# A decoder trunk on one core: address phases of the matmul operands in SBUF

## The chip, the core and the metric

The kernel runs on one core of one Trainium2 chip. The metric is the device time of one execution in microseconds (us), from which the host is left out; the profile is one such execution, taken by the hardware profiler. A smaller number is better.

## The reference

Two decoder layers over 256 tokens of width 2048, in float32: layer 0 mixes tokens with retention (8 heads), layer 1 with sliding-window attention (32 heads, 4 of keys and values). Each mixer is followed by a SwiGLU block and by a gated per-layer embedding; one last norm ends it.

```python
for i in range(DEPTH):                       # 2 layers, 256 tokens, d = 2048
    h = rmsnorm(x, norm_mix[i])
    if i % 2 == 0:
        x = x + retention_mixer(h, ret_w_in[j], ret_gn[j], ret_w_out[j])
    else:
        x = x + swa_mixer(h, swa_w_in[j], swa_sinks[j], swa_w_out[j])
    x = x + swiglu(rmsnorm(x, norm_ffn[i]), ffn_w_in[i], ffn_w_out[i])
    gate = jax.nn.sigmoid(rmsnorm(x, norm_ple[i]) @ ple_w_gate[i])
    x = x + gate * (p[i] @ ple_w_proj[i])
return rmsnorm(x, norm_final)
```

Nearly all of the arithmetic is the projections: an activation of 256 tokens times a weight matrix that is read from HBM once.

## The kernel before, in words

Every projection is cut into chunks of 512 output columns, and each chunk into units of 256 rows of the weight (two blocks of 128 rows, 128 x 1024 values in SBUF). 928 such units go by in one fixed order, from the first projection of layer 0 to the last of layer 1, with 12 matmuls to a unit.

For a unit, four things happen on four engines. The SyncE queue loads the weights into a `raw` buffer (five of them, `load`, L130). ScalarE rounds them to float32r into a `hi` buffer (L208). VectorE puts the remainder into a `lo` buffer (L209). TensorE then multiplies (`multiply`, L141 to L161). Loads run five units ahead, the splits three units ahead (`run`, L163), and there are four `hi` and four `lo` buffers, so that the buffer of unit i + 3 is the one that unit i - 1 has left. In between, steps of side work (transposes, norms, attention) are put into the engines' queues.

The activation is the stationary operand. It too lies in two float32r parts, each transposed to [128, blocks, 256 tokens]: `xTh` and `xTl` for the residual stream (the operand of every projection that reads a norm), `pTh` and `pTl` for the embedding, and tiles of a stage's own pool for the inputs of the output projections: `yTh`/`yTl` (retention), `oTh`/`oTl` (attention), `hTh`/`hTl` (SwiGLU). For each block and each half of the tokens there are three matmuls of 128 x 128 by 128 x 512, in this order: stationary `xTh` with moving `hi` (L159), the same `xTh` with moving `lo` (L160), `xTl` with moving `hi` (L161). Each has a weight load of its own (PEld, 128 x 128), and the load for the next matmul runs while the present one streams.

Three places need a name for what follows. A tile's *phase* is its start address in the partition modulo 128 bytes. The blocks of a stationary tile are 512 bytes wide and those of a moving tile 2048 bytes, so every operand of L159 to L161 has the phase of its tile. The built program's allocation gives for the kernel before:

| tile | start, bytes | phase |
|---|---|---|
| `xTh`, `xTl` | 33952, 50336 | 32, 32 |
| `pTh`, `pTl` | 66720, 68768 | 32, 32 |
| `raw`, five | 70816 to 87200 | 32 |
| `hi`, four | 91296 to 103584 | 32 |
| `lo`, four | 107680 to 119968 | 32 |
| `yTh`, `oTh`, `hTh` (each in its stage) | 132288 | 64 |
| `yTl`, `oTl`, `hTl` | 165056, 148672, 177344 | 64 |
| `prh`, `prl`, `vh`, `vl` (retention's inner products, L350 to L352) | 209600 to 216768 | 64 |

So a projection that reads `xT` or `pT` has stationary and moving operands of one phase, and one that reads `yT`, `oT` or `hT` has its stationary operand 32 bytes further on.

Of the kernel before, what the change touches and what calls it, by code (L numbers as in the profile page):

```python
# [2 lines left out]

# [8 lines left out]
F32 = mybir.dt.float32  # L12
# [6 lines left out]
P = 128  # L19
D = 2048  # L20
S = 256
# [22 lines left out]
class Lhs:  # L44
    """A transposed activation, split exactly into two float32r parts."""

# [8 lines left out]
class Chunk:  # L55
    """512 output columns for all tokens, accumulated over the whole contraction, in pieces of
    a token tile and some of the columns."""

# [6 lines left out]
class Unit:  # L65
    """KU blocks of 128 rows of a weight, in one chunk's columns."""

# [5 lines left out]
class Stage:  # L73
    """A part of the trunk with tiles of its own, from its first unit to its last."""

# [3 lines left out]
    def linear(self, w, block, lhs, done, units=None, chunk=None):  # L79
        """One chunk: block of 512 columns of a weight laid out by `_units`."""  # L80
        ch = chunk or Chunk(self, done)
        for u in units if units is not None else range(w.shape[1]):
            self.units.append(Unit(ch, w[block, u], range(KU * u, KU * u + KU), lhs))
            ch.left += 1
# [3 lines left out]
def tile_trunk(ctx, tc, ins, out):  # L88
    nc = tc.nc
    pool = ctx.enter_context(tc.tile_pool(name="persist", bufs=1))  # L90
    wraw = ctx.enter_context(tc.tile_pool(name="wraw", bufs=5))
    whi = ctx.enter_context(tc.tile_pool(name="whi", bufs=4))
    wlo = ctx.enter_context(tc.tile_pool(name="wlo", bufs=4))
    small = ctx.enter_context(tc.tile_pool(name="small", bufs=4))
# [9 lines left out]
    turned = ctx.enter_context(tc.tile_pool(name="turned", bufs=1))  # L104
    xT = [pool.tile([P, KD, S], F32R, name=n) for n in ("xTh", "xTl")]
    pT = [pool.tile([P, PLE_K, S], F32R, name=n) for n in ("pTh", "pTl")]

    # ---------------------------------------------------------------- streams
    side = deque()

    def step_side():
# [21 lines left out]
    def split_weights(u):  # L133
        raw = u.w
        hi = whi.tile([P, KU, NW], F32R, name="hi")
        lo = wlo.tile([P, KU, NW], F32R, name="lo")
        for part in u.parts:
            split(hi[:, part, :], lo[:, part, :], raw[:, part, :])
        u.w = (hi, lo)

    def multiply(u, which, left):  # L141
        """The unit's products for some pieces of its chunk; `left` of the chunk's units are
        still to come."""
        ch = u.chunk
        need(u.lhs, u.kts)
        if ch.acc is None:
            ch.acc = []
            for n, (_, cols) in enumerate(ch.pieces):
                bank, name = (ps_acc, "acc") if n < NT else (ps_at, "at")
                ch.acc.append(bank.tile([P, NW], F32, name=name)[:, : cols.stop - cols.start])  # L150
        hi, lo = u.w
        for j, k in enumerate(u.kts):
            first = not ch.begun and j == 0
            last = left == 0 and j == KU - 1
            for n in which:
                t, cols = ch.pieces[n]
                sl = slice(t * P, (t + 1) * P)
                xh, xl = u.lhs.hi[:, k, sl], u.lhs.lo[:, k, sl]
                nc.tensor.matmul(ch.acc[n], xh, hi[:, j, cols], start=first, stop=False)  # L159
                nc.tensor.matmul(ch.acc[n], xh, lo[:, j, cols], start=False, stop=False)  # L160
                nc.tensor.matmul(ch.acc[n], xl, hi[:, j, cols], start=False, stop=last)  # L161

    def run(stages, begin):  # L163
        """All units in order, their weights AHEAD units ahead; between them, steps of side work.
        The products of the units that end the last chunk go piece by piece of its output."""
        units = [(st, u) for st in stages for u in st.units]
# [37 lines left out]

    # ------------------------------------------------------------ small pieces
    def split(hi, lo, src, scale=None):
# [9 lines left out]
    def transpose_pair(srcs):  # L216
        """Two [128, 128] blocks of both token tiles -> a PSUM tile [128, 2, S]."""
        tr = ps_tr.tile([P, 2, S], F32, name="tr")
        for j, pair in enumerate(srcs):
            for t in range(NT):  # L220
                nc.tensor.transpose(tr[:, j, t * P : (t + 1) * P], pair[t], ident)
        return tr

    def transposes(dst, src):
        """Steps that transpose src [128, NT, 512] into dst [128, 4, S], by blocks of 32 x 32."""
        n = P // SQ
        src = src.rearrange("p t (k c f) -> p t k c f", c=n, f=SQ)
        dst = dst.rearrange("p k (t c f) -> p t k c f", c=n, f=SQ)
        for i in range(n * n):
            if i % STEP == 0:  # L230
                yield
            a, b = divmod(i, n)
            nc.vector.transpose(  # L233
                dst[b * SQ : (b + 1) * SQ, :, :, a, :], src[a * SQ : (a + 1) * SQ, :, :, b, :]
            )

    def blocks(src, i):
        """Blocks 2i and 2i + 1 of 128 columns of both token tiles."""
        return [[src(t)[:, b * P : (b + 1) * P] for t in range(NT)] for b in (2 * i, 2 * i + 1)]

    class Norm:
        """Sums of squares of the residual's chunks, and the transposed residual times the gain.
        The scale by token, inv, is applied behind the product with the weights."""

# [22 lines left out]
        def places(self, c, src):  # L267
            """Steps that put a chunk's four transposed blocks in place."""
            for j in range(4):
                if j % 2 == 0:  # L270
                    yield
                self.place(4 * c + j, src[:, j, :])
# [5 lines left out]
    def residual(stage, norm, c):  # L278
        """A chunk of an output projection onto the residual, then the next norm's part."""

# [14 lines left out]

    # --------------------------------------------------------------- retention
    def retention(norm, next_norm, w_in, w_out):
# [97 lines left out]

    # ---------------------------------------------------- sliding-window attention
    def swa(norm, next_norm, w_in, w_out):
# [36 lines left out]
        def q_done_of(j):  # L434
            def q_done(acc):
# [12 lines left out]
                def scores(i):  # L448
                    """Of heads 2i and 2i + 1: the numerators and denominators' parts."""
                    ats = [ps_at.tile([P, 3 * P], F32, name="at") for _ in range(2)]  # L450
# [97 lines left out]
        for j in range(SKV):  # L548
            stage.linear(w_in, j, norm.lhs, q_done_of(j))
        # The first chunks' last units wait for the last group of heads.  # L550
        n = KD // KU
# [7 lines left out]

    # --------------------------------------------------------------------- FFN  # L560
    def ffn(layer, norm, next_norm):
# [57 lines left out]

    # --------------------------------------------------------------------- PLE  # L620
    def ple(layer, norm, next_norm, final):
# [12 lines left out]
        def pair(c):  # L634
# [3 lines left out]
            def gate_done(acc):  # L638
# [7 lines left out]
                def later():  # L646
                    # The last reads of the old operand are queued: its place is free.
                    for b, xt in enumerate(st["xt"]):
                        yield from next_norm.places(b, xt)
# [34 lines left out]
            def gate_last(acc, t, cols):  # L684
                """A piece of the last chunk; with a token tile's last one, its rows go out."""
                fin, rest, row = st["fin"], st["rest"], xs[:, t, :]
# [37 lines left out]

    # ------------------------------------------------------------------- trunk
    norms = [Norm(w, layer) for layer in range(DEPTH) for w in range(3)] + [Norm(None, 0)]
# [14 lines left out]
    def load_x():  # L741
        """The first norm's operand comes transposed, in step with the first chunk's weights."""
        for b in range(KD // KU):
# [19 lines left out]
def _constants():  # L763
    """Tables that follow from the shapes alone."""
    h = np.arange(RH, dtype=np.float64)
# [14 lines left out]
def _units(w):  # L780
    """[K, N] -> [N / 512, K / 256, 128, 2, 512]: each unit in one piece, by partitions."""
    k, n = w.shape
    return w.reshape(k // (KU * P), KU, P, n // NW, NW).transpose(3, 0, 2, 1, 4)


def _heads(w):
    """The retention's columns by heads: q and k, v, g."""
    q, k, v, g = np.split(w, [RH * RK, 2 * RH * RK, 2 * RH * RK + RH * RV], axis=1)
    parts = [a.reshape(D, RH, -1) for a in (q, k, v, g)]
    return np.concatenate(parts, axis=2).reshape(D, -1)  # L790
# [44 lines left out]
```

## Time and profile before

| what | value |
|---|---|
| time, median of 3 runs | 2649.82 us (2649.51 to 2650.46) |
| span of the profiled execution | 2647.9 us |
| TensorE busy in it | 2629.2 us, 99% |
| VectorE, ScalarE busy | 1817.2 us, 1223.7 us |
| granted TensorE clock, mean | 0.999 |
| 128 x 512 matmuls with stationary `xT` or `pT` | 7728 + 96 = 7824 |
| with stationary `yT`, `oT` or `hT` | 768 + 384 + 2112 = 3264 |
| HBM read | 493.63 MB, 187 GB/s over the span |

The profiled execution's own time is its span and what lies around it: the median of the runs is 1.9 us over the span. In the rows of the profile, a group is given by its source line, engine, operation and tiles (out<-in, with the moving operand or the stationary one first, as the program names them), then its count, its busy time and the mean duration of one instruction in ns. A matmul's duration overlaps the next one's, since matmuls are pipelined; what a matmul costs is the distance from one start to the next, which a window's length over its count of matmuls gives.

### The profile page before, as it was taken

How to read it: one execution, taken by the hardware profiler on the slowest of the kernel's cores; microseconds unless marked ns; L12 is line 12 of the kernel's file. 1: busy time of each engine (PE TensorE's matmuls, PEld its weight loads, DVE VectorE, ACT ScalarE, POOL GpSimd, SP SyncE). 2: the span in 40 equal slices, each digit the busy share in tenths (PEclk: the TensorE clock that was granted, in tenths of full speed). 3: DMA queues.
4: the chain of work that ended last, by engine and by line, in shares of the span. 5: the costliest groups of instructions: out<-in, count | busy, mean ns of one | idle time of the engine just before them, and what ended most of it. 6: DMA issues, size and time to landing. Idle time of an engine off the chain costs nothing.

```text
span 2647.9 us, 31279 instructions
## 1 busy us (share of the span) xinstructions
PE 2629.2 (99%) x11632; PEld 2142.7 (81%) x11632; DVE 1817.2 (69%) x2567; ACT 1223.7 (46%) x1527; POOL 14.6 (1%) x30
## 2 busy tenths in 40 slices
PE   8999999999999999999999999999999999999998
PEld 6888888888888888888888887777888888888887
DVE  6777777766666667676555786888757575755565
ACT  6444444444444444444444555555444444444444
POOL 0000000000000000000000000000000000000000
PEclk9999999999999999999999999999999999999999
DMA  8555555565566565656655655346666666555564
GB/s 277 185 185 186 185 186 183 181 190 184 194 192 193 191 197 190 198 186 197 190 187 187 190 193 169 121 135 202 189 198 189 197 194 194 192 188 187 189 207 144
DMA packets 140506, 497.79 MB, mean 188 GB/s; under 512 B 15809, under 2 KB 19009, under 8 KB 140225
## 3 DMA queue, kind: packets, MB, share of 16 engines
q1 hardware_dynamic: 140064, 495.73, 58.5%
q8 instruction: 91, 1.49, 0.2%
q14 instruction: 63, 0.51, 0.1%
q10 hardware_dynamic: 288, 0.07, 0.0%
HBM read 493.63 MB, written 2.10 MB: 187 GB/s over the span
## 4 chain that ended last, share of the span: by engine, by line
PE 95%; DVE 3%; issue 1%; DMA 1%; ACT 0%; SPq 0%; ACTq 0%; POOLq 0%; POOL 0%; DVEq 0%
PE acc L159 31%; PE acc L161 31%; PE acc L160 31%; DVE lo L209 1%; DVE xt L233 1%; PE at L454 1%; PE tr L506 0%; PE at L532 0%; DMA raw<-in_ret_w_in 0%; PE at L323 0%; DVE xTl L212 0%; DVE qkT L233 0%; DMA xs<-in_x 0%; PE at L350 0%; PE at L352 0%
## 5 line engine op out<-in xcount | busy, mean ns | idle before, releaser
L209 DVE TENSOR_TENSOR lo<-raw,hi 128x1024 fp32r<-128x1024 f32 (+1 forms) x929 | 1131.8, 1221 | 720.2 <-ACT hi L208 712.8
L208 ACT ACTIVATE hi<-raw 128x1024 fp32r<-128x1024 f32 (+1 forms) x929 | 982.0, 1058 | 1210.9 <-PE acc L161 1117.4
L159 PE MATMUL acc<-hi,xTh 128*128 128x512 f32 x2592 | 1011.0, 390 | 6.6 <-ACT hi L208 5.4
L161 PE MATMUL acc<-hi,xTl 128*128 128x512 f32 x2592 | 1008.0, 389 | 0.8 <-DVE xTl L212 0.6
L160 PE MATMUL acc<-lo,xTh 128*128 128x512 f32 x2592 | 1008.7, 389 | 0.0
L159 PEld LDWEIGHTS acc<-hi,xTh 128*128 128x128 f32 x2592 | 487.3, 188 | 111.6 <-ACT hi L208 5.6
L161 PEld LDWEIGHTS acc<-hi,xTl 128*128 128x128 f32 x2592 | 487.0, 188 | 103.6 <-DVE xTl L212 2.5
L160 PEld LDWEIGHTS acc<-lo,xTh 128*128 128x128 f32 x2592 | 487.3, 188 | 100.5 <-issue 0.7
L161 PE MATMUL acc<-hi,hTl 128*128 128x512 f32 x704 | 278.4, 396 | 0.0
L160 PE MATMUL acc<-lo,hTh 128*128 128x512 f32 x704 | 278.4, 395 | 0.0
L159 PE MATMUL acc<-hi,hTh 128*128 128x512 f32 x704 | 278.4, 395 | 0.0
L233 DVE STREAM_TRANSPOSE xt<-h 32x256 f32<-32x256 f32 x352 | 153.6, 436 | 6.8
L161 PEld LDWEIGHTS acc<-hi,hTl 128*128 128x128 f32 x704 | 132.2, 188 | 32.1
L160 PEld LDWEIGHTS acc<-lo,hTh 128*128 128x128 f32 x704 | 132.2, 188 | 32.1
L159 PEld LDWEIGHTS acc<-hi,hTh 128*128 128x128 f32 x704 | 132.2, 188 | 31.9
L233 DVE STREAM_TRANSPOSE xt<-xs 32x256 f32<-32x256 f32 x320 | 139.5, 436 | 6.0
L161 PE MATMUL acc<-hi,yTl 128*128 128x512 f32 x256 | 101.2, 396 | 0.0
L160 PE MATMUL acc<-lo,yTh 128*128 128x512 f32 x256 | 101.2, 395 | 0.0
L159 PE MATMUL acc<-hi,yTh 128*128 128x512 f32 x256 | 101.2, 395 | 0.0
L233 DVE STREAM_TRANSPOSE qkT<-qk 32x256 f32<-32x256 f32 x128 | 55.8, 436 | 10.2 <-ACT qk L315 8.1
L211 ACT ACTIVATE xTh<-xt,gains 128x256 fp32r<-128x256 f32 x80 | 35.8, 499 | 56.0 <-DVE xt L233 51.6
L159 PEld LDWEIGHTS acc<-hi,yTh 128*128 128x128 f32 x256 | 48.1, 188 | 11.7
(124 smaller groups left out, 1178.2 us busy)
## 6 DMA issues: line engine op xcount, KB each, us to landing
raw<-in_ffn_w_in SPq DMA_DIRECT2D x352, 512.0 KB, 4.2
raw<-in_ret_w_in SPq DMA_DIRECT2D x191, 512.0 KB, 3.6
raw<-in_ffn_w_out SPq DMA_DIRECT2D x176, 512.0 KB, 4.0
raw<-in_ret_w_out SPq DMA_DIRECT2D x64, 512.0 KB, 4.0
raw<-in_ple_w_gate SPq DMA_DIRECT2D x64, 512.0 KB, 3.8
raw<-in_swa_w_in SPq DMA_DIRECT2D x40, 512.0 KB, 3.7
raw<-in_swa_w_out SPq DMA_DIRECT2D x32, 512.0 KB, 3.7
raw<-in_ple_w_proj SPq DMA_DIRECT2D x8, 512.0 KB, 4.0
```

The costliest lines, as they stand in the source:

```text
L159: nc.tensor.matmul(ch.acc[n], xh, hi[:, j, cols], start=first, stop=False)
L160: nc.tensor.matmul(ch.acc[n], xh, lo[:, j, cols], start=False, stop=False)
L161: nc.tensor.matmul(ch.acc[n], xl, hi[:, j, cols], start=False, stop=last)
L208: nc.scalar.activation(hi, src, AF.Copy)
L209: nc.vector.tensor_tensor(lo, src, hi.bitcast(F32), op=ALU.subtract)
L211: nc.scalar.activation(hi, src, AF.Copy, scale=scale)
L233: nc.vector.transpose(dst[b * SQ : (b + 1) * SQ, :, :, a, :], src[a * SQ : (a + 1) * SQ, :, :, b, :])
L454: nc.tensor.matmul(ats[e][:, 0:P] if b == 0 else ats[e][:, P : 3 * P], qT[sl, i, b * P : (b + 1) * P], kT[sl, j, 0 : (b + 1) * P], start=True,
```

## The change

Only addresses change. The `hi` and `lo` buffers leave their rotating pools and become eight fixed tiles, used in turn by a counter (the pools also handed out four buffers in turn). Small tiles that nothing reads are put between them as pads: 96 bytes ahead of `xTh`, 32 bytes between `xTh` and `xTl`, and 32 bytes behind each `hi` buffer. On every engine the instructions, their order and the semaphores that each waits for are those of before; docstrings and some comments go too, and L159 becomes L169, L208 becomes L218.

```diff
     pool = ctx.enter_context(tc.tile_pool(name="persist", bufs=1))
     wraw = ctx.enter_context(tc.tile_pool(name="wraw", bufs=5))
-    whi = ctx.enter_context(tc.tile_pool(name="whi", bufs=4))
-    wlo = ctx.enter_context(tc.tile_pool(name="wlo", bufs=4))
...
-    xT = [pool.tile([P, KD, S], F32R, name=n) for n in ("xTh", "xTl")]
+    pool.tile([P, 24], F32, name="pad0")
+    xT = [pool.tile([P, KD, S], F32R, name="xTh")]
+    pool.tile([P, 8], F32, name="pad1")
+    xT.append(pool.tile([P, KD, S], F32R, name="xTl"))
     pT = [pool.tile([P, PLE_K, S], F32R, name=n) for n in ("pTh", "pTl")]
+    whi_at, wlo_at = [], []
+    for tiles, name in ((whi_at, "hi"), (wlo_at, "lo")):
+        for n in range(4):
+            tiles.append(pool.tile([P, KU, NW], F32R, name=f"{name}{n}"))
+            if name == "hi":
+                pool.tile([P, 8], F32, name=f"pad_hi{n}")
...
     def split_weights(u):
         raw = u.w
-        hi = whi.tile([P, KU, NW], F32R, name="hi")
-        lo = wlo.tile([P, KU, NW], F32R, name="lo")
+        at = next(turn)
+        hi, lo = whi_at[at % 4], wlo_at[at % 4]
```

The allocation of the changed program, with the tiles that keep their phase in the last rows:

| tile | start, bytes | phase before | phase now |
|---|---|---|---|
| `xTh` | 34048 | 32 | 0 |
| `hi0` | 70944 | 32 | 32 |
| `hi1` | 75072 | 32 | 64 |
| `hi2` | 79200 | 32 | 96 |
| `hi3` | 83328 | 32 | 0 |
| `xTl`, `pTh`, `pTl` | 50464, 66848, 68896 | 32 | 32 |
| `lo0` to `lo3` | 87456 to 99744 | 32 | 32 |
| `raw`, five | 103840 to 120224 | 32 | 32 |
| `yT`, `oT`, `hT`, `pr`, `v` | from 132544 on | 64 | 64 |

More of the change, by code (lines that the diff above doesn't have):

```diff
@@ L2 @@
 from contextlib import ExitStack
+from itertools import count
 import numpy as np
@@ L104, in tile_trunk @@
     turned = ctx.enter_context(tc.tile_pool(name="turned", bufs=1))
-    xT = [pool.tile([P, KD, S], F32R, name=n) for n in ("xTh", "xTl")]
+    pool.tile([P, 24], F32, name="pad0")
+    xT = [pool.tile([P, KD, S], F32R, name="xTh")]
+    pool.tile([P, 8], F32, name="pad1")
+    xT.append(pool.tile([P, KD, S], F32R, name="xTl"))
     pT = [pool.tile([P, PLE_K, S], F32R, name=n) for n in ("pTh", "pTl")]
+    whi_at, wlo_at = [], []
[4 more added lines that the diff above has]
+                pool.tile([P, 8], F32, name=f"pad_hi{n}")
     side = deque()
+    turn = count()
     def step_side():
```

## The prediction

> **What bounds the kernel now.** First the page of the profile: the span, the busy time of TensorE, the clock it was granted, and the chain that ended last.
>
> ```profile
> span 2647.9 us, 31279 instructions
> PE 2629.2 (99%) x11632; PEld 2142.7 (81%) x11632; DVE 1817.2 (69%) x2567; ACT 1223.7 (46%) x1527; POOL 14.6 (1%) x30
> PEclk9999999999999999999999999999999999999999
> PE 95%; DVE 3%; issue 1%; DMA 1%; ACT 0%; SPq 0%; ACTq 0%; POOLq 0%; POOL 0%; DVEq 0%
> ```
>
> TensorE is the bound from end to end, at full clock. It waits for hardly anything, so the time is the number of matmuls times the distance from one start to the next. Second, then, the busy time by stretches. The columns are the stretch, its length, and for PE, PEld, DVE, ACT and POOL the busy time with the count of instructions, then clock and DMA. The rows are the retention's output projection (stationary `yT`), the first SwiGLU's input projection (`xT`) and its output projection (`hT`).
>
> ```profile
> 562.60:741.80 179.20, 179.20 (x769) 144.29 (x768) 117.98 (x154) 78.96 (x95) 0.00 (x0) 1.00 0.59 190
> 741.80:1220.50 478.70, 478.70 (x2113) 396.52 (x2112) 318.45 (x401) 213.83 (x226) 0.70 (x1) 1.00 0.61 193
> 1220.50:1466.90 246.40, 246.40 (x1057) 198.37 (x1057) 146.03 (x175) 102.49 (x114) 0.00 (x0) 1.00 0.59 188
> ```
>
> The same matmul of 128 x 128 by 128 x 512 has two prices. With `xT` it is 478.70 / 2112 = 226.7 ns, with `hT` 246.40 / 1056 = 233.3 ns, with `yT` 179.20 / 768 = 233.3 ns (the odd one in each count lies on the edge). TensorE never idles in these stretches and the clock is 1.00 in all. With `xT` both operands start at phase 32; with `hT` and `yT` the stationary operand starts at 64 and the moving one at 32. That is what the change touches.
>
> Third, the groups of matmuls inside a steady stretch, 800 to 1200 us with `xT` and 1240 to 1440 us with `hT` (count, busy time, mean ns of one).
>
> ```profile
> L159 PE MATMUL acc<-hi,xTh 128*128 128x512 f32 x589 | 229.1, 389 | 0.0
> L161 PE MATMUL acc<-hi,xTl 128*128 128x512 f32 x589 | 229.1, 389 | 0.0
> L159 PE MATMUL acc<-hi,hTh 128*128 128x512 f32 x286 | 113.1, 396 | 0.0
> L161 PE MATMUL acc<-hi,hTl 128*128 128x512 f32 x286 | 113.1, 396 | 0.0
> ```
>
> A recorded duration is the distance to the next start plus about 162 ns: 389 goes with 226.7, 396 with 233.3. So the distance can be read from the duration of a single matmul, also where stages mix.
>
> Fourth, the timeline at 59.8 us, where the retention's inner products (all operands at phase 64, L350 to L352) come in between the `xT` matmuls, and the same few matmuls by group.
>
> ```profile
> 60.02 0.40 PE L161 MATMUL acc<-hi,xTl 128*128 128x512 f32 x1
> 60.25 0.39 PE L350 MATMUL at<-vh,prh 128*128 128x512 f32 x1
> 60.48 0.39 PE L351 MATMUL at<-vl,prh 128*128 128x512 f32 x1
> 60.71 0.39 PE L352 MATMUL at<-vh,prl 128*128 128x512 f32 x1
> 60.94 0.39 PE L159 MATMUL acc<-hi,xTh 128*128 128x512 f32 x1
> 61.17 0.40 PE L160 MATMUL acc<-lo,xTh 128*128 128x512 f32 x1
> 61.40 0.39 PE L161 MATMUL acc<-hi,xTl 128*128 128x512 f32 x1
> 61.63 0.39 PE L159 MATMUL acc<-hi,xTh 128*128 128x512 f32 x1
> ...
> 62.99 0.39 PE L159 MATMUL acc<-hi,xTh 128*128 128x512 f32 x1
> ```
>
> ```profile
> L161 PE MATMUL acc<-hi,xTl 128*128 128x512 f32 x1 | 0.4, 397 | 0.0
> L352 PE MATMUL at<-vh,prl 128*128 128x512 f32 x1 | 0.4, 393 | 0.0
> L350 PE MATMUL at<-vh,prh 128*128 128x512 f32 x1 | 0.4, 391 | 0.0
> L351 PE MATMUL at<-vl,prh 128*128 128x512 f32 x1 | 0.4, 387 | 0.0
> ```
>
> From 60.02 to 61.63 us lie 7 distances, 230 ns on average; from 61.63 to 62.99 lie 6, back at 226.7. The single ones run from 387 to 397 ns, that is 225 to 235 ns apart. So 226.7 ns is a state that the stream settles into when the phases stay alike, and a change of phase puts it out for about seven matmuls, above the settled price on average.
>
> **The change part by part.** Call *offset* the phase of the stationary tile whose load runs, less that of the moving tile that streams beside it. Before, it is 0 with `xT` and `pT` (226.7 ns) and 32 with `yT`, `oT`, `hT` (233.3 ns); 64 and 96 do not occur in a projection. Afterwards `xTh` stands at 0 and the four `hi` at 32, 64, 96 and 0, so in the `xT` stages the offset beside a moving `hi` is 96, 64, 32 and 0 in four successive units, while beside `lo` (32) it stays 0, since the load is then that of `xTl` (32). In the `yT`, `oT` and `hT` stages it is 32, 0, 96 and 64 beside `hi`, and 32 beside `lo` as before. Within a unit the phases alternate as well, two matmuls with `hi` to one with `lo`.
>
> *The `xT` and `pT` stages, 7824 matmuls.* Three units in four, 5868 matmuls, leave offset 0. Their price is not in the trace in this mixture. The nearest row is the mixed stretch above, 230 ns, which lies between the settled 226.7 and the settled 233.3 of offset 32; I take it: 5868 x (230 - 226.7) = +19.4 us. The fourth unit has offset 0 throughout, but it comes from a unit that has not: of its 12 matmuls I count 3 at 230 until it settles, 163 units x 3 x 3.3 ns = +1.6 us. In the 96 `pT` matmuls among these the order of the four differs, which changes nothing of weight.
>
> *The `yT`, `oT` and `hT` stages, 3264 matmuls.* Three units in four, 2448 matmuls, leave offset 32 beside `hi`, and I price them at the same 230 ns: 2448 x (230 - 233.3) = -8.1 us. The fourth stays.
>
> *Bounds.* Known are offset 32 and offset 0. Beside `hi` stand 2/3 of the matmuls, 1304 per buffer in the `xT` stages and 544 in the others. Were the two unseen offsets as quick as the quickest matmul of the mixed stretch (387 ns, 225 ns apart), the sum is 1304 x 6.6 - 2608 x 1.7 = +4.2 us in the `xT` stages and -544 x 6.6 - 1088 x 8.3 = -12.6 us in the others, -8.4 us together. Were they as slow as the slowest (397 ns, 235 ns), it is 1304 x 6.6 + 2608 x 8.3 = +30.3 us and -544 x 6.6 + 1088 x 1.7 = -1.7 us, +28.6 us together; with the 1956 `lo` matmuls of those units drawn along to 230, 6.5 us more.
>
> *ScalarE and VectorE*, which now write `hi` at other phases: nothing in the trace shows that price, in either direction, but they have cover.
>
> ```profile
> L208 ACT ACTIVATE hi<-raw 128x1024 fp32r<-128x1024 f32 x927 | 980.8, 1059 | 1209.4 <-PE acc L161 1117.4 <-issue 64.3 <-ACT hi L208 10.3
> L209 DVE TENSOR_TENSOR lo<-raw,hi 128x1024 fp32r<-128x1024 f32 x927 | 1130.5, 1222 | 718.7 <-ACT hi L208 711.4
> L159 PE MATMUL at<-hi,xTh 128*128 128x256 f32 x16 | 4.5, 283 | 0.0
> ```
>
> A unit takes TensorE 12 x 226.7 = 2720 ns, against 1059 ns of ScalarE and 1222 ns of VectorE, and ScalarE spends 1117.4 us waiting for TensorE to leave a `hi` buffer. Were either engine 10% slower at a new phase, the wait would shrink and nothing else; I count zero. Without that cover it would be 0.1 us for each of the 927 in the row, 93 us. The fixed buffers in turn add no wait and no instruction, and no queue is passed; zero.
>
> *Sum:* 19.4 + 1.6 - 8.1 = +12.9 us. Against the profiled execution, 2647.9 + 12.9 = 2660.8 us of span; the median stands 1.9 us over the span, so 2649.8 + 12.9 = 2662.7 us, +0.5%.
>
> A rule of the Trainium skill speaks against any effect at all: SBUF — State Buffer, section "Who interferes with whom", has contention only at the port pair that VectorE and GpSimd share, gives TensorE one read port for the moving operand and another for the weight load, and says "PE and ACT never wait on anyone". By it the sum would be 0. The trace agrees in that no engine's activity moves the 226.7 ns, and disagrees in that the same matmul costs 226.7 and 233.3 ns at the same clock.
>
> **The rivals.**
>
> *The phase is not what sets the price.* In the trace, phase and place go together: `xT` lies below 67 KB, `yT`, `oT` and `hT` above 132 KB, and the moving tiles at 91 to 124 KB. If the place is what costs 6.6 ns, the change, which moves no matmul operand by more than 21 KB and none across to the other side, does nothing: 2649.8 us. For it: the 128-byte phase is only one of the differences, and the page named above knows none of the kind. Against it: the `pr` and `v` tiles lie above 209 KB at equal phases and give distances on both sides of 226.7, and price steps of single ns at equal places show that fine alignment of the two streams matters.
>
> *The unseen offsets are the good ones.* The trace has a 128 x 256 matmul as well, 283 ns in the row above, so 121 ns apart; 256 more columns take 226.7 - 121 = 106 ns, 512 take 212, and some 15 ns of each matmul is not streaming. If that part is the two reads getting in each other's way, offset 64, with the reads half a period apart, might be free of it, and 96 as well. At 225 ns for both, the sum of the bounds above holds: 2649.8 - 8.4 = 2641.4 us. With only offset 64 free of all 15 ns (212 ns) and 96 at 230: 1304 x (6.6 + 3.3 - 14.7) = -6.3 us and 544 x (-6.6 - 3.3 - 21.3) = -17.0 us, 2626.5 us. It decides for faster as soon as the two unseen offsets together average under about 227 ns, since the `xT` stages lose 1304 x 6.6 = 8.6 us at offset 32 and the others gain 3.6 us at offset 0. For it: one matmul in the mixed stretch does run at 225. Against it: it is followed by 231, the mean is 230, and of the two offsets known the aligned one is the better.
>
> **How the numbers follow.** The forecast, a mixture that costs more than the settled state: 0.59. No effect of the phase: 0.18. Unseen offsets that are better: 0.23. A measurement of this kernel can tell about 0.2%, 5.3 us, from no change. Slower by more than that is nearly all of the first case and none of the others, 0.57; within it the second case and the edges of the first and third, 0.22; faster by more the rest of the third, 0.21. The range has the unseen offsets at their slow bound on top, 2649.8 + 28.6 = 2678.4 us, and takes in the second case and the milder form of the third, down to 2639 us; about a tenth is left out below it and less above.
>
> **What would show it.** In the changed profile the matmuls at the lines of `hi` and `lo` with `xT` should have a mean near 392 ns where they had 389, and those with `hT` and `yT` near 394 where they had 396; a stretch of the first SwiGLU's input projection should hold its 2112 matmuls in about 485 us instead of 478.7, and its output projection in about 244 instead of 246.4. Every fourth unit should come close to 226.7 ns. Means of 389 and 396 as before would make the place the cause. A mean under 389 with `xT` would make the prediction wrong, and so would a row of ScalarE or VectorE that ends TensorE's waits.

## The result and the profile after

The changed kernel takes 2686.15 us (median, 2685.17 to 2686.58), the kernel before 2649.9 us beside it: a ratio of 1.0135, 95% interval 1.0122 to 1.0147, slower by 36.3 us. Slower was forecast, but by 12.9 us, and 2686 lies above the top of the range, 2678.4.

The page of the changed kernel, in the lines that were shown of before:

```profile
span 2683.3 us, 31279 instructions
PE 2665.1 (99%) x11632; PEld 2142.3 (80%) x11632; DVE 1817.3 (68%) x2567; ACT 1223.8 (46%) x1527; POOL 14.6 (1%) x30
PEclk9999999999999999999999999999999999999999
PE 95%; DVE 2%; issue 1%; DMA 1%; ACT 0%; SPq 0%; ACTq 0%; POOLq 0%; POOL 0%; DVEq 0%
```

The count of instructions, the clock and the busy time of the other engines are those of before. Only TensorE is busy for longer, by 35.9 us, which is the whole of the span's 35.4. The same stretches as before, now at their new places (retention's output projection, first SwiGLU's input projection, its output projection):

```profile
574.01:752.27 178.26, 178.26 (x770) 144.24 (x769) 117.83 (x154) 78.92 (x95) 0.00 (x0) 1.00 0.62 190
752.27:1242.43 490.16, 490.16 (x2114) 396.42 (x2112) 318.42 (x401) 213.75 (x226) 0.70 (x1) 1.00 0.61 189
1242.43:1487.52 245.09, 245.09 (x1057) 198.32 (x1056) 145.81 (x175) 102.53 (x114) 0.00 (x0) 1.00 0.62 189
```

With stationary `xT`, 2112 matmuls take 490.16 us where they took 478.70: 232.1 ns apart, 5.4 more than before. With `yT` and `hT` they are 178.26 / 768 = 232.1 and 245.09 / 1056 = 232.1 ns apart, 1.2 less. All stages now have one price. Scaled up, 7824 x 5.4 - 3264 x 1.2 ns = +38 us, 3 more than the span shows.

ScalarE, which writes `hi` at the new phases (count, busy time, mean ns, idle time before it):

```profile
L218 ACT ACTIVATE hi<-raw 128x1024 fp32r<-128x1024 f32 x927 | 980.5, 1058 | 1251.7 <-PE acc L171 1147.7 <-issue 76.9 <-ACT hi L218 11.8
```

It writes as fast as before (1058 ns against 1059) and waits for TensorE a little longer.

Last, the timeline of the changed kernel, cut down to the first matmul of five units in a row, whose moving tiles are `hi0`, `hi1`, `hi2`, `hi3` and `hi0` again:

```profile
908.23 0.39 PE L169 MATMUL acc<-hi,xTh 128*128 128x512 f32 x1
...
911.02 0.39 PE L169 MATMUL acc<-hi,xTh 128*128 128x512 f32 x1
...
913.79 0.39 PE L169 MATMUL acc<-hi,xTh 128*128 128x512 f32 x1
...
916.59 0.40 PE L169 MATMUL acc<-hi,xTh 128*128 128x512 f32 x1
...
919.37 0.39 PE L169 MATMUL acc<-hi,xTh 128*128 128x512 f32 x1
```

Twelve matmuls take 2.79, 2.77, 2.80 and 2.78 us, 232.5, 230.8, 233.3 and 231.7 ns each. The fourth unit, whose `hi3` has `xTh`'s phase and which was to settle at 226.7, lies among the others. Averaged over all units of a buffer in the stretch with `xT` (from the starts in the trace), it is 233.1, 230.9, 233.0 and 231.4 ns.

### The profile page after: what moved, and what is told of

It reads as the page before. It is cut to its first block, busy times and chain, and to the rows that moved or that the text cites. A ratio compares the mean times of both kernels' runs of the same rounds, so it can differ in the third digit from the quotient of the medians.

```text
span 2683.3 us, 31279 instructions
## 1 busy us (share of the span) xinstructions
PE 2665.1 (99%) x11632; PEld 2142.3 (80%) x11632; DVE 1817.3 (68%) x2567; ACT 1223.8 (46%) x1527; POOL 14.6 (1%) x30
## 4 chain that ended last, share of the span: by engine, by line
PE 95%; DVE 2%; issue 1%; DMA 1%; ACT 0%; SPq 0%; ACTq 0%; POOLq 0%; POOL 0%; DVEq 0%
PE acc L170 31%; PE acc L169 31%; PE acc L171 31%; DVE lo L219 1%; DVE xt L243 1%; PE at L464 1%; PE tr L516 0%; PE at L542 0%; DMA raw<-in_ret_w_in 0%; PE at L333 0%; DMA xs<-in_x 0%; DVE qkT L243 0%; PE at L361 0%; PE at L360 0%; PE at L362 0%
## 5 line engine op out<-in xcount | busy, mean ns | idle before, releaser
L218 ACT ACTIVATE hi<-raw 128x1024 fp32r<-128x1024 f32 (+1 forms) x929 | 981.7, 1058 | 1252.9 <-PE acc L171 1147.7
L169 PE MATMUL acc<-hi,xTh 128*128 128x512 f32 x2592 | 1023.2, 395 | 6.5 <-ACT hi L218 5.4
L170 PE MATMUL acc<-lo,xTh 128*128 128x512 f32 x2592 | 1022.9, 395 | 0.0
L169 PEld LDWEIGHTS acc<-hi,xTh 128*128 128x128 f32 x2592 | 487.2, 188 | 128.4 <-ACT hi L218 5.9
L169 PE MATMUL acc<-hi,hTh 128*128 128x512 f32 x704 | 277.6, 394 | 0.0
L169 PEld LDWEIGHTS acc<-hi,hTh 128*128 128x128 f32 x704 | 132.4, 188 | 31.3
L169 PE MATMUL acc<-hi,yTh 128*128 128x512 f32 x256 | 100.9, 394 | 0.0
L243 DVE STREAM_TRANSPOSE qkT<-qk 32x256 f32<-32x256 f32 x128 | 55.8, 436 | 10.8 <-ACT qk L325 8.7
L243 DVE STREAM_TRANSPOSE xt<-y 32x256 f32<-32x256 f32 x128 | 55.9, 437 | 2.5
```

The lines of the kernel that those rows point to most:

```text
L218: nc.scalar.activation(hi, src, AF.Copy)
L243: nc.vector.transpose(dst[b * SQ : (b + 1) * SQ, :, :, a, :], src[a * SQ : (a + 1) * SQ, :, :, b, :])
```

## The experiments

Theory at this point: the pads alone cost the time, 226.7 ns needs operands that lie alike from matmul to matmul, and any mixture loses it. Rivals: the fixed buffers or their new places cost it; or each offset has a price of its own, which a matmul pays whatever its neighbours do. In the tables of offsets below, an offset is the start of the stationary tile less that of the moving one modulo 256 bytes, for reasons that the runs give. Each kernel here was run once, but for the aligned one (four times); seven runs of the kernel before lay between 2648.8 and 2652.1 us, so a difference of a few us says nothing.

### Which part of the change costs it

**No pads.** The changed kernel without `pad0`, `pad1` and `pad_hi`.

```diff
-    pool.tile([P, 24], F32, name="pad0")
...
-    pool.tile([P, 8], F32, name="pad1")
...
-            if name == "hi":
-                pool.tile([P, 8], F32, name=f"pad_hi{n}")
```

> The changed kernel without its pads: fixed hi and lo buffers in turn, and every operand at phase 32 again (the stage tiles at 64), as before the change. Theory 'phases' (the pads alone cost the 36 us): 2649.8 us, 226.7 ns from matmul to matmul with xT, 233.3 ns with hT. Rival 'place and buffers' (fixed buffers, or where they now lie, 20 KB lower, cost it): about 2686 us and 231 to 232 ns with xT.

Measured: 2649.84 us, against 2650.46 for the kernel before on the same chip. First SwiGLU's input and output projection:

```profile
742.31:1221.05 478.74, 478.74 (x2114) 396.53 (x2113) 318.54 (x401) 213.83 (x226) 0.70 (x1) 1.00 0.59 193
1221.05:1467.44 246.39, 246.39 (x1057) 198.36 (x1056) 146.02 (x175) 102.49 (x114) 0.00 (x0) 1.00 0.58 188
```

226.7 and 233.3 ns again. The fixed buffers, 20 KB lower, cost nothing; the pads cost it all.

**The activation's pads alone.** `pad_hi` taken out, `pad0` and `pad1` left.

```diff
-            if name == "hi":
-                pool.tile([P, 8], F32, name=f"pad_hi{n}")
```

> Of the pads only those of the activation: xTh at phase 0, xTl, hi and lo all at 32. The same three pairs of phases return in every triple of matmuls. Theory 'mixture' (the settled 226.7 ns needs one pair of phases from matmul to matmul, a change inside the triple breaks it for all three): all three matmuls with xT near 231.6 ns, 7824 x 4.9 ns = +38 us, 2688 us. Rival 'price by offset' (each matmul pays for its own offset, whatever its neighbours): the matmul with lo, whose offset is 0, stays at 226.7, those with hi take the 232.5 ns of the changed kernel at this offset, 5216 x 5.8 ns = +30 us, 2680 us. Rival 'place': 2649.8 us.

Measured: 2697.43 us against 2650.46. First SwiGLU's input projection:

```profile
755.95:1248.75 492.80, 492.80 (x2113) 396.35 (x2112) 318.61 (x401) 213.55 (x226) 0.70 (x1) 1.00 0.58 188
```

With `xT` 492.80 / 2112 = 233.3 ns, above both expectations, and +47 us: half of the change costs more than all of it. Two in three matmuls had their offset changed, yet the loss is 3 x 6.6 ns per triple, as if all three had. That speaks against a price for each matmul by its own offset.

**The weights' pads alone.** `pad0` and `pad1` taken out, `pad_hi` left.

```diff
-    pool.tile([P, 24], F32, name="pad0")
...
-    pool.tile([P, 8], F32, name="pad1")
```

> Of the pads only those of the hi buffers: hi at 32, 64, 96 and 0 in turn, xTh, xTl and lo at 32. Theory 'mixture': the unit whose hi stands at 32 settles to 226.7, in the other three all matmuls run near 231.6, 5868 x 4.9 ns = +29 us less 2 us in the hT stages, about 2677 us. Rival 'price by offset': the matmul with lo stays at 226.7 in all units, those with hi cost what their offset costs in the changed kernel, about +24 us, 2674 us; the lo matmuls tell the two apart. Rival 'place': 2649.8 us.

Measured: 2683.92 us against 2650.46.

```profile
752.60:1242.17 489.57, 489.57 (x2114) 396.45 (x2113) 318.57 (x401) 214.00 (x226) 0.70 (x1) 1.00 0.58 189
1242.17:1487.26 245.09, 245.09 (x1057) 198.33 (x1056) 145.81 (x175) 102.65 (x114) 0.00 (x0) 1.00 0.59 189
```

231.8 ns with `xT`, 232.1 with `hT`, and more in all than either expectation. Both of those had matmuls that stay aligned. But the four pads of 32 bytes also move `lo` by 128, and by the period of 256 bytes that the next runs show, no unit here is aligned throughout. Each half of the change by itself destroys the settled state, and the two do not add up.

### Constant offsets

Four kernels leave the kernel before as it is but for a pad behind `pTl`, which sets the offset of all matmuls with `xT`, and one ahead of the stage tiles, which sets that of all with `yT`, `oT` and `hT` (one of the four has only the second pad). A fifth moves everything. Nothing mixes within a stage.

```diff
     turned = ctx.enter_context(tc.tile_pool(name="turned", bufs=1))
+    turned.tile([P, 24], F32, name="pad3")
...
     pT = [pool.tile([P, PLE_K, S], F32R, name=n) for n in ("pTh", "pTl")]
+    pool.tile([P, 24], F32, name="pad2")
```

**96 and 96 bytes** (the diff above): offsets 160 and 128.

> The kernel before with one pad of 96 bytes behind pTl and one of 96 bytes ahead of the stage tiles, so that nothing mixes: xT stays at 32 and hi and lo stand at 0 (offset 32 in all matmuls with xT), hT, yT, oT stand at 0 as well (offset 0). Theory 'phases': the two prices change sides, 233.3 ns with xT and 226.7 ns with hT, 7824 x 6.6 - 3264 x 6.6 ns = +30 us, 2680 us. Rival 'place' (tiles above 132 KB are the dear ones): 226.7 with xT, 233.3 with hT, 2649.8 us.

Measured: 2697.89 us against 2650.46.

```profile
755.71:1248.51 492.80, 492.80 (x2113) 396.44 (x2112) 318.62 (x401) 213.63 (x226) 0.69 (x1) 1.00 0.58 188
1248.51:1494.91 246.40, 246.40 (x1057) 198.20 (x1056) 146.04 (x175) 102.64 (x114) 0.00 (x0) 1.00 0.59 188
```

Half of the expectation held. With `xT` the price went from 226.7 to 233.3, and no `xT` tile had moved, only what it is multiplied with: the place of the stationary tile is not what sets it. But `hT`, now at `hi`'s phase modulo 128, stayed at 233.3. Equal phases of 128 bytes are not enough.

**0 and 224 bytes:** `xT` as before, `hT` at offset 0 modulo 256.

> The kernel before with one pad of 224 bytes ahead of the stage tiles: hT, yT and oT now start at a multiple of 256 bytes from hi and lo, as xT always did, and nothing else moves. Theory 'one aligned state' (226.7 ns belongs to operands a multiple of 256 bytes apart in every matmul, all else runs at 233.3 or mixes): 226.7 ns in all stages, 3264 x 6.6 ns less, 2628 us. Rival 'the place of the stage tiles costs it' or a period of 512 bytes (hT stands 256 bytes off modulo 512): 233.3 ns with hT stays, 2649.8 us.

Measured: 2630.29 us, ratio 0.9928, 95% interval 0.9911 to 0.9944: faster than both kernels.

```profile
736.45:1215.17 478.72, 478.72 (x2113) 396.53 (x2112) 318.46 (x401) 213.82 (x226) 0.70 (x1) 1.00 0.61 193
1215.17:1454.53 239.36, 239.36 (x1057) 198.26 (x1056) 145.79 (x175) 102.23 (x114) 0.00 (x0) 1.00 0.61 194
```

239.36 / 1056 = 226.7 ns with `hT`. One unused tile of 224 bytes moved 3264 matmuls by 6.6 ns, 21.5 us by the sum and 19.7 us measured. With the run before, it puts the period at 256 bytes: a difference of 128 does not give the state, one of 256 does.

**32 and 32 bytes**, then **64 and 64:** the offsets that were left.

> The kernel before with a pad of 32 bytes behind pTl and one of 32 bytes ahead of the stage tiles: constant offsets that have not been seen, 224 (modulo 256) with xT and 64 with hT, yT, oT. Theory 'one aligned state': 233.3 ns in all stages, 7824 x 6.6 ns = +52 us, 2701 us. Rival 'price by offset' (each offset has a price of its own, as the 229 to 236 ns in the changed kernel look): some other number than 233.3 in at least one of the two, down to 225 ns.

> The same with 64 and 64 bytes: constant offsets 192 with xT and 96 with hT, yT, oT. Theory 'one aligned state': 233.3 ns in all stages, 2701 us. Rival 'price by offset': another number than 233.3 in at least one of the two.

Measured: 2698.18 and 2667.57 us, the kernel before 2649.95. First the one with 32 bytes:

```profile
756.10:1248.90 492.80, 492.80 (x2113) 395.87 (x2112) 318.39 (x401) 213.72 (x226) 0.70 (x1) 1.00 0.59 188
1248.90:1495.30 246.40, 246.40 (x1057) 197.47 (x1056) 146.13 (x175) 102.42 (x114) 0.00 (x0) 1.00 0.60 188
```

Then the one with 64:

```profile
746.84:1230.26 483.42, 483.42 (x2113) 396.66 (x2112) 318.61 (x401) 213.74 (x226) 0.70 (x1) 1.00 0.60 192
1230.26:1477.66 247.40, 247.40 (x1057) 198.89 (x1056) 146.23 (x175) 102.53 (x114) 0.00 (x0) 1.00 0.60 187
```

The theory fails in the second. Offsets 224 and 64 give 233.3 ns as it said, but offset 192 gives 483.42 / 2112 = 228.9 ns and offset 96 gives 247.40 / 1056 = 234.3. So there is not one good state and one bad price; the steps of 32 bytes, held constant, have these prices (32 to 128 were seen with `hT` alone, 160 to 224 with `xT` alone; the second SwiGLU gives the same as the first within 0.2 ns):

| offset modulo 256 | 0 | 32 | 64 | 96 | 128 | 160 | 192 | 224 |
|---|---|---|---|---|---|---|---|---|
| ns from matmul to matmul | 226.7 | 233.3 | 233.3 | 234.3 | 233.3 | 233.3 | 228.9 | 233.3 |

**All of it 64 bytes further on.** Offset 0 everywhere, at another phase (64 bytes ahead of `xTh`, 224 ahead of the stage tiles).

```diff
     turned = ctx.enter_context(tc.tile_pool(name="turned", bufs=1))
+    turned.tile([P, 56], F32, name="pad3")
+    pool.tile([P, 16], F32, name="pad1")
```

> All operands of all projections a multiple of 256 bytes apart as in u5_all_aligned, and all of them 64 bytes further on. Theory 'only the difference counts': 226.7 ns in all stages, 2630 us. Rival 'the phase itself counts too': another price in all stages, up to 233.3 ns, 2703 us.

Measured: 2630.56 us against 2650.62.

```profile
736.63:1215.35 478.72, 478.72 (x2114) 396.40 (x2113) 318.50 (x401) 213.82 (x226) 0.70 (x1) 1.00 0.59 193
1215.35:1454.71 239.36, 239.36 (x1058) 198.20 (x1057) 145.79 (x175) 102.22 (x114) 0.00 (x0) 1.00 0.61 194
```

226.7 ns throughout, at a second phase: here too the differences count, and not the phase itself.

### Mixtures

**`lo` alone off.** A pad of 224 bytes between the `hi` and the `lo` buffers, in the kernel before.

```diff
     whi = ctx.enter_context(tc.tile_pool(name="whi", bufs=4))
+    between = ctx.enter_context(tc.tile_pool(name="between", bufs=1))
+    between.tile([P, 56], F32, name="pad_lo")
     wlo = ctx.enter_context(tc.tile_pool(name="wlo", bufs=4))
```

> The kernel before with one pad of 224 bytes between the hi and the lo buffers. hi, xT and now hT, yT, oT are a multiple of 256 bytes apart; lo alone stands off by 32, in all stages. Theory 'the state needs every matmul': one off in three takes all three out, 233.3 ns in all stages, 2701 us. Rival 'price by offset': two in three at 226.7 and the one with lo at 233.3, mean 228.9, 7824 x 2.2 - 3264 x 4.4 ns = +3 us, 2653 us.

Measured: 2682.6 us against 2649.95. The input projection of the first SwiGLU, then that of the second in two parts, all with the same addresses and the same matmuls:

```profile
748.92:1237.02 488.10, 488.10 (x2113) 397.05 (x2112) 318.49 (x401) 213.79 (x226) 0.70 (x1) 1.00 0.60 190
1831.09:1847.73 16.64, 16.64 (x74) 13.40 (x72) 15.74 (x27) 8.12 (x13) 0.69 (x1) 1.00 0.55 169
1849.13:2324.43 475.30, 475.30 (x2039) 382.43 (x2037) 303.37 (x374) 206.18 (x214) 0.00 (x0) 1.00 0.60 189
```

The first SwiGLU runs at 488.10 / 2112 = 231.1 ns, and the second begins so too, 16.64 / 72 = 231.1. Then TensorE waits for VectorE, which writes the last part of `xTl`:

```profile
1848.79 0.50 PE L163 MATMUL acc<-hi,xTl 128*128 128x512 f32 x1 [0.38 <-DVE xTl L214]
```

From there on it is 475.30 / 2037 = 233.3 ns. The same pattern can run at two prices, then, and a short wait changed one into the other.

In the first SwiGLU (800 to 1200 us) the two matmuls with `hi`, whose offset is 0, do not both keep the settled 389 ns of duration:

```profile
L163 PE MATMUL acc<-hi,xTl 128*128 128x512 f32 x577 | 227.8, 395 | 0.0
L161 PE MATMUL acc<-hi,xTh 128*128 128x512 f32 x577 | 225.3, 390 | 0.0
```

One operand in three that lies off makes matmuls dearer that are themselves aligned. That and the mean, 231.1 to 233.3 ns where a price for each matmul by its own offset gives 228.9, rule out such a price.

**`lo` and `xTl` moved together** by 32 bytes.

```diff
+    between = ctx.enter_context(tc.tile_pool(name="between", bufs=1))
+    between.tile([P, 8], F32, name="pad_lo")
...
+    xT = [pool.tile([P, KD, S], F32R, name="xTh")]
+    pool.tile([P, 8], F32, name="pad1")
+    xT.append(pool.tile([P, KD, S], F32R, name="xTl"))
...
+    pool.tile([P, 56], F32, name="pad2")
```

> The kernel before with xTl and lo both moved on by 32 bytes, xTh and hi left (pads between them). A matmul's own operands now differ in two of three (xTh with lo, xTl with hi), but the weight load that runs beside a stream always reads a tile a multiple of 256 bytes from the streaming one: xTh loads beside hi, xTl beside lo. Theory 'the load beside the stream': 226.7 ns with xT as before; with hT, yT, oT offsets 64 and 32 mix, 231 to 234 ns, 2643 to 2653 us in all. Rival 'a matmul's own operands': a mixture with xT, 231 to 234 ns, 7824 x 4.3 to 7.3 ns more, 2684 to 2707 us.

Measured: 2685.68 us against 2650.62. Input and output projection of the first SwiGLU, then the output projection of the second:

```profile
754.39:1244.84 490.45, 490.45 (x2113) 396.56 (x2112) 318.56 (x401) 213.84 (x226) 0.70 (x1) 1.00 0.58 189
1244.84:1491.24 246.40, 246.40 (x1057) 198.08 (x1056) 146.12 (x175) 102.49 (x114) 0.00 (x0) 1.00 0.58 188
2330.25:2574.31 244.06, 244.06 (x1058) 198.35 (x1057) 145.78 (x175) 102.52 (x114) 0.00 (x0) 1.00 0.60 190
```

232.2 ns with `xT`. The plainest mechanism, a weight load that meets the stream beside it, falls in the form in which it was stated: each load was aligned with the stream beside it, and the state was lost. Price and time are those that the rival, a matmul's own operands, forecast; it is not shown by that alone, since `hi` and `lo`, and `xTh` and `xTl`, were moved apart as well. With `hT` the same addresses ran at 233.3 ns in the first SwiGLU and at 244.06 / 1056 = 231.1 in the second.

**One aligned unit in four.** Of the changed kernel's pads only those of `hi`, and 128 bytes more that bring `lo` back to `xT`, so that the units of `hi0` have all operands at offset 0.

```diff
-    pool.tile([P, 24], F32, name="pad0")
...
-    pool.tile([P, 8], F32, name="pad1")
...
+        if name == "hi":
+            pool.tile([P, 32], F32, name="pad_lo")
```

> Of the pads only those of the hi buffers, and one more that brings lo back to xTh and xTl: every fourth unit (hi0) has all its operands aligned for 12 matmuls on end, the other three have hi at 32, 64 and 96 further. The prediction's step 'the fourth unit settles within about three more matmuls': 226.7 ns in most of that unit, a mean near 227.5. Rival 'twelve matmuls are too few': about 231 ns there too. The other units mix, 231 to 233 ns. With the step right about 2676 us, with the rival about 2686 us.

Measured: 2680.21 us against 2649.72. The timeline from the start of such a unit, its fourth matmul, and the starts of the next units:

```profile
907.33 0.40 PE L169 MATMUL acc<-hi,xTh 128*128 128x512 f32 x1
907.56 0.40 PE L170 MATMUL acc<-lo,xTh 128*128 128x512 f32 x1
907.80 0.39 PE L171 MATMUL acc<-hi,xTl 128*128 128x512 f32 x1
908.03 0.39 PE L169 MATMUL acc<-hi,xTh 128*128 128x512 f32 x1
...
910.07 0.40 PE L169 MATMUL acc<-hi,xTh 128*128 128x512 f32 x1
...
912.87 0.39 PE L169 MATMUL acc<-hi,xTh 128*128 128x512 f32 x1
```

Three matmuls take 0.70 us, the nine behind them 2.04 us, 226.7 ns each: a unit that is aligned modulo 256 does settle after three matmuls, and by the trace all 44 such units of this stretch do. The three cost more than was expected (0.70 / 3 = 233 ns), so the unit's mean is 228.3 in place of 227.5, and the total lies between the two forecasts. The next unit runs at 2.80 / 12 = 233.3.

**Sixteen bytes.** `xT` 16 bytes behind an aligned place, `yT`, `oT` and `hT` 16 bytes ahead of one. A further pad sets the stage tiles right, and a scratch tile of the norms has one buffer in place of two.

```diff
+    turned.tile([P, 48], F32, name="pad3")
...
+    def pushed(pool, k, name):
+        t = pool.tile([P, k * S + 8], F32R, name=name, bufs=1)
+        pool.tile([P, 56], F32, name="pad_" + name, bufs=1)
+        return t[:, 4 : 4 + k * S].rearrange("p (k s) -> p k s", k=k)
...
+    xT = [pushed(pool, KD, n) for n in ("xTh", "xTl")]
```

> A step finer than the allocator gives: xT starts 16 bytes behind an aligned place, hT, yT and oT 16 bytes ahead of one (offsets 16 and 240), pT stays aligned, and one small scratch tile has one buffer in place of two to make room. Theory 'an exact multiple is needed': 233.3 ns in all stages, 2701 us. Rival 'near is enough' (both starts lie in one stretch of 32 bytes at offset 16): 226.7 with xT, 233.3 with hT, 2650 us. A third outcome is a better place than the aligned one: under 226.7 in either.

Measured: 2664.85 us against 2650.62. Input and output projection of the first SwiGLU, then the output projection of the second:

```profile
752.28:1245.07 492.79, 492.79 (x2114) 399.06 (x2113) 318.60 (x401) 213.90 (x226) 0.70 (x1) 1.00 0.58 188
1245.07:1486.19 241.12, 241.12 (x1057) 198.11 (x1056) 145.75 (x175) 102.53 (x114) 0.00 (x0) 1.00 0.60 192
2315.30:2554.66 239.36, 239.36 (x1057) 198.20 (x1056) 145.81 (x175) 102.55 (x114) 0.00 (x0) 1.00 0.60 194
```

None of the three outcomes. At offset 240 the price is 228.3 ns in layer 0 and 226.7 in layer 1. At offset 16 it is 233.3 in the first SwiGLU, and it changes twice later on, at unmoved addresses. The first time is in the gated embedding of layer 0, where 12 aligned matmuls with `pT` (the middle row) come between two stretches of 96 with `xT`:

```profile
1486.19:1508.58 22.39, 22.39 (x97) 18.14 (x96) 19.45 (x32) 11.86 (x17) 0.70 (x1) 1.00 0.58 187
1508.58:1511.33 2.75, 2.75 (x14) 2.25 (x12) 0.41 (x1) 2.74 (x4) 0.00 (x0) 1.00 0.61 198
1511.33:1533.09 21.76, 21.76 (x98) 18.02 (x96) 19.71 (x29) 10.41 (x14) 0.00 (x0) 1.00 0.57 182
```

It is 22.39 / 96 = 233.2 ns ahead of them and 21.76 / 96 = 226.7 behind them. The second time is in the input projection of the second SwiGLU, around two waits for `xT`, of 0.90 us and, a microsecond later, 0.38 us (the first is shown):

```profile
1834.27:1850.84 16.57, 16.57 (x72) 13.42 (x71) 14.53 (x25) 8.00 (x11) 0.69 (x1) 1.00 0.53 171
1852.13 0.50 PE L166 MATMUL acc<-hi,xTh 128*128 128x512 f32 x1 [0.90 <-ACT xTh L218]
1853.58:2315.30 461.72, 461.72 (x2038) 382.32 (x2037) 303.25 (x375) 206.41 (x214) 0.00 (x0) 1.00 0.60 195
```

Ahead of it 71 matmuls take 233.4 ns each, behind it 461.72 / 2037 = 226.7. So near the aligned place the stream can run in the good state or outside it, and it stays as it is until something disturbs it; at offset 0 it reached the good state in every stretch shown here.

## Why the prediction was wrong, point by point

**What bounds the kernel** held: TensorE from end to end, and the time is the count of matmuls times their distance. ScalarE and VectorE were costed at nothing, and cost nothing (1058 ns, and more waiting).

**The sign and its cause** held. The settled 226.7 ns is lost in the `xT` stages, and the other stages gain a little; the place rival (0.18), which forecast no change, fell with the result and with the two runs that moved the price by a pad alone, and the rival of good unseen offsets (0.23) fell with the result.

**The step that failed** is "The fourth unit has offset 0 throughout ... I count 3 at 230 until it settles". Its mechanism was right: in the run with one aligned unit in four it takes three matmuls. Its premise was wrong: the period is 256 bytes, and modulo 256 `hi3` lies 128 bytes from `xTh`, and `lo` 128 from `xTl`. No unit of the changed kernel is aligned, and the fourth runs at 231.7 ns. It was costed at +1.6 us for 1956 matmuls; at 231.7 it costs 1956 x 5.0 = +9.8 us. The trace of before could not tell 128 from 256, since its only offsets were 0 and 32; the prediction took 128 as if it could. By the size of its miss this step is the second, 8.2 of 25 us.

**The mixture's price** was mis-sized, and that is the largest part of the miss. "I take it: 5868 x (230 - 226.7)" rested on seven matmuls at one place; in the timeline above, the three units that mix take 232.5, 230.8 and 233.3 ns, 232.2 on average, and 5868 x 5.5 = +32.3 us in place of 19.4. In the other stages the same gave -8.1 us, and 3264 x 1.2 = -4 us came. These sums add up to +38 us where +12.9 was forecast: 12.9 us of the 25 between come from the mixture with `xT`, 8.2 from the fourth unit and 4.1 from the other stages. The measured span grew by 35.4, 3 less than the sum, as above.

**The upper bound** was worked out from 235 ns for the two unseen offsets alone, with one in three matmuls (`lo`) left at the settled price and, as an extra, 6.5 us if not. All of them were drawn along, by as much as the others; the 6.5 us stood in the text and not in the range, and at the measured price it is 1956 x 5.5 = 10.8 us. It belonged in the range. With the 6.5 us the top would have been 2684.9, still a little below the 2686.15 measured; with 10.8 it would have been 2689.2.

**The page that spoke against any effect.** The Trainium skill, SBUF — State Buffer, section "Who interferes with whom", says that TensorE never waits on anyone at SBUF and that its two read ports are independent. Here a pad of 224 bytes that nothing reads made the kernel faster by 19.7 us, at the same clock and with the same instructions, so the measurement decides: the relative addresses of the two operands do cost TensorE time.

**What stays open** is the mechanism. That the load of the next stationary tile and the stream of the present moving one meet in SBUF would explain a price by difference of addresses, but in its simple form it did not pass the run with `lo` and `xTl` moved together. A conflict of each matmul's own two operands fits that run, but no run moved them alone. That history matters is shown by unmoved addresses at two prices within one stage; why 12 aligned matmuls or a wait of under 1 us change the state, and why the wait made the stream quicker in one run and slower in another, is not. Which offsets below 32 bytes always settle was not tried beyond 16 and 240.

## What to carry to other kernels

Where TensorE is the bound, read the distance from one matmul to the next stage by stage, not only its busy share: two prices for one shape at one clock mean that something about the operands differs, here their start addresses modulo 256 bytes. Put all stationary and all moving tiles of a stream at the same address modulo 256; here one pad of 224 bytes gave 0.7%. A stream that changes its pattern every few instructions is priced by its mixtures, so price it from a long stretch that mixes in the same way, or state the bounds with every neighbour drawn along.

## What the runs showed of the hardware that was not expected

- The same matmuls at the same addresses ran at 233.3 and at 226.7 ns within one stage (offset 16), and at 231.1 and 233.3 with `lo` off. The change came at a wait of TensorE of under 1 us, or behind 12 aligned matmuls: the distance depends on what the stream went through before.
- Seven of the eight constant offsets in steps of 32 bytes lie above 226.7, five of them at 233.3 ns, but 192 at 228.9 and 96 at 234.3: the price is not a smooth function of the distance.
- A mixture can be cheaper than a constant bad offset: with `xT` the whole change runs at 232.1 ns, offset 160 or 224 held constant at 233.3.
